# Rotary embedding on one core: cutting the last batch's store into 16, 12 and 4 KB a row, with the 4 KB in two DMAs of 126 and 2 partitions

## The chip, the cores and the metric

The kernel runs on one core of a Trainium2 chip. The metric is the device time of one execution in microseconds (us). Before the change it is 163.42 us, the median of three runs (163.31 to 163.57). The profile is one further execution, with a hardware profiler; its own time is 163.25 us, of which 161.4 us is the span from the first to the last instruction.

## The reference

Each head's 64 numbers are split into two halves of 32, and the halves are rotated by an angle that belongs to the position in the sequence. The input `x` is 8 x 2048 x 8 x 64 in float32, 33.5 MB; `cos` and `sin` are 2048 x 32.

```python
def reference(x, cos, sin):
    x1 = x[..., : x.shape[-1] // 2]
    x2 = x[..., x.shape[-1] // 2 :]
    cos = cos[None, :, None, :]
    sin = sin[None, :, None, :]
    out1 = x1 * cos - x2 * sin
    out2 = x1 * sin + x2 * cos
    return np.concatenate([out1, out2], axis=-1)
```

Each input number is read once and each output number written once, so some 67 MB cross between the device memory (HBM) and the on-chip memory, against a handful of multiplications and additions for each.

## The kernel before

**Layout.** A batch of `x` is laid over the 128 partitions: partition q holds 16 consecutive positions (`R`), each of 8 x 64 = 512 numbers (`HD`). One row, that is one partition of one batch, is 8192 numbers or 32 KB (`ROW`), contiguous in HBM and on the chip. `UNIT` is four positions, 8 KB a row. A whole batch is 4 MB.

**Loads.** Five buffers hold a batch each. `load` (line 64) puts the load of a batch on the queue of SyncE (SP), as one DMA of 32 KB a row, except that the first batch comes in 8, 8 and 16 KB a row. The load of batch b + 5 is issued after the work on batch b has been put in order (line 192), and SP waits before it until the store of batch b has left the buffer.

**Work.** `rotate` (line 101) handles one piece of a batch, 8 KB a row as a rule. In the common kind, "A", GpSimd (POOL) multiplies the swapped halves by `sin` and its negative (line 121), VectorE (DVE) multiplies the piece by `cos` (line 128) and adds the two in place (line 135). In five pieces, listed at line 98, the sum is made by TensorE with an identity matrix and copied back by ScalarE (ACT). None of these are in the last batch.

**Stores.** `shares` (line 176) says in which cuts a batch is stored, `pieces` (line 169) in which cuts it is computed. The main loop (line 183) computes a piece and then issues every store whose numbers are all done. `store` (line 70) puts it on the queue of ACT, but for the last batch on that of SP, whose loads are over by then. The last batch is computed in five pieces of 8, 8, 8, 4 and 4 KB a row, and stored in three cuts of 16, 8 and 8 KB a row: after the second piece, after the third, and after the fifth.

**Order.** `keep` keeps the marked instructions of an engine in the order in which they are written, so no scheduler moves them. Between engines and DMAs the order is made by semaphores. A DMA adds sixteen steps to its semaphore in all, as the transfer engines that carry its parts report. The program ends when the landings of all stores have been waited for, at the `TileContext`'s end.

**DMA.** A DMA is a list of rows. The sixteen transfer engines of the core carry it; the DMAs of SP and of ACT are two queues (q1 and q10 in the profile) on the same sixteen engines. In this kernel before the change every DMA has 128 rows. One row of a DMA shows in the trace as one packet; each of the sixteen engines carries eight rows.

Of the kernel before, what the change touches and what calls it, by code (L numbers as in the profile page):

```python
# [10 lines left out]
def kernel(  # L11
# [8 lines left out]
    keep = tc.keep_in_program_order  # L20
# [5 lines left out]
    P = 128  # L26
    HD = H * D
    R = S // P
    ROW = R * HD
    UNIT = 4 * HD  # L30
    NBUF = 5
    C = 512
    last = B - 1

    xv = x.rearrange("b (q r) h d -> b q (r h d)", q=P)
    ov = out.rearrange("b (q r) h d -> b q (r h d)", q=P)
# [19 lines left out]
    xts = {}  # L56
# [12 lines left out]

    def store(b, lo, n):  # L70
        queue = nc.sync if b == last else nc.scalar
        keep(queue.dma_start(out=ov[b, :, lo : lo + n], in_=xts[b][:, lo : lo + n]))

    keep(nc.scalar.dma_start(out=sin_sb, in_=sin_src))
    keep(nc.sync.dma_start(out=cos_sb, in_=cos_src))  # L75
# [3 lines left out]
    for mat, one in ((eye, 1.0), (neye, -1.0)):  # L79
        nc.gpsimd.memset(mat, 0.0)  # L80
        nc.gpsimd.affine_select(
            out=mat,
            in_=mat,
# [92 lines left out]
    def shares(b):  # L176
        if b == 0:
            return [2 * HD, 6 * HD, 2 * UNIT]
        if b == last:
            return [2 * UNIT, UNIT, UNIT]  # L180
        return [ROW]

    for b in range(B):
        done = 0
        outs = list(spans(shares(b)))
        for lo, n in spans(pieces(b)):
            rotate(b, lo, n)
            done = lo + n
            while outs and sum(outs[0]) <= done:
                store(b, *outs.pop(0))  # L190
        if b + NBUF <= last:
            load(b + NBUF)
# [30 lines left out]
```

## Time and profile before

| what | us |
|---|---|
| median of the runs (range) | 163.42 (163.31 to 163.57) |
| profiled execution | 163.25 |
| its span | 161.4 |
| busy in the span: DVE | 141.0 |
| busy in the span: POOL | 139.4 |
| busy in the span: PE (matmul) | 47.3 |
| busy in the span: ACT | 11.4 |
| busy share of the 16 DMA engines: q1 (SP) | 55.2% |
| busy share of the 16 DMA engines: q10 (ACT) | 42.7% |
| moved between HBM and chip | 67.65 MB, mean 419 GB/s |

The page cuts the span into 40 equal slices of about 4 us, and gives for each how busy the engines were and how much the DMA engines moved. The rows on DMA issues give the time from the issue of a transfer by its queue to its landing. The timeline lists the instructions with their start and length, in us from the start of the span. The view by stretches gives, for any stretch of the span, the busy time of PE, PEld, DVE, ACT and POOL, then the granted clock of TensorE, the mean busy share of the DMA engines and the GB/s that they moved. Below these views lie the packet records, one for each row that a transfer engine moved, with its queue, start, length and bytes, but without the number of the engine; and the times of the single semaphore steps.

### The profile page before, as it was taken

The page shows a single profiled execution, that of the slowest core. Times are in us where ns is not written, and L with a number is a line of the kernel's source. Part 1 is how long each engine was busy: PE and PEld are TensorE (multiplying, and loading weights), DVE is VectorE, ACT ScalarE, POOL GpSimd, SP SyncE. Part 2 cuts the span into 40 slices and gives each one's busy share as a digit, 9 for nine tenths or more (in the row PEclk, how much of TensorE's full clock was granted, in tenths as well). Part 3 has the DMA queues.
Part 4 walks back from the last instruction along what each step waited for, and adds up shares of the span by engine and source line. Part 5 has one row for each costly group of instructions (what it writes and reads, how often), then busy time and mean ns, then how long its engine had stood idle before and what let it go on. Part 6 is the DMA issues. An engine that isn't in the chain of part 4 may idle for free.

```text
span 161.4 us, 462 instructions
## 1 busy us (share of the span) xinstructions
PE 47.3 (29%) x80; PEld 17.9 (11%) x80; DVE 141.0 (87%) x68; ACT 11.4 (7%) x11; POOL 139.4 (86%) x72
## 2 busy tenths in 40 slices
PE   0000000397408770779029721974000000000000
PEld 0000000132003220223013301420000000000000
DVE  0668899999999999999999999999999998999900
ACT  0000000032200220020100220022000000000000
POOL 2299999999999899998995999998999979999200
PEclk9999999999975998589957995599655555555555
DMA  4999999999999999999999999999999999999995
GB/s 159 426 447 434 420 436 447 414 406 503 390 390 455 455 455 390 463 447 390 463 447 390 449 455 400 430 463 406 430 463 406 430 463 406 430 463 394 418 404 229
DMA packets 3458, 67.65 MB, mean 419 GB/s; under 512 B 384, under 2 KB 384, under 8 KB 768
## 3 DMA queue, kind: packets, MB, share of 16 engines
q1 hardware_dynamic: 2016, 38.01, 55.2%
q10 hardware_dynamic: 1440, 29.62, 42.7%
q14 instruction: 2, 0.02, 0.0%
HBM read 34.08 MB, written 33.55 MB: 419 GB/s over the span
## 4 chain that ended last, share of the span: by engine, by line
DVE 53%; DMA 27%; POOL 9%; issue 5%; SPq 0%; DVEq 0%; POOLq 0%
DVE t L128 28%; DMA xt<-in_x_dram 27%; DVE xt L135 22%; POOL t L121 9%; DVE t L147 3%; SPq L75 0%; DVEq L135 0%; POOLq L121 0%; SPq L67 0%
## 5 line engine op out<-in xcount | busy, mean ns | idle before, releaser
L121 POOL TENSOR_TENSOR t<-xt,sin_sb 128x1024 f32<-128x1024 f32 (+1 forms) x32 | 70.4, 2201 | 10.3 <-DMA xt<-in_x_dram 7.9
L128 DVE TENSOR_TENSOR t<-xt,cos_ps 128x2048 f32<-128x2048 f32 (+1 forms) x34 | 73.4, 2166 | 1.9 <-DMA xt<-in_x_dram 1.1
L121 POOL TENSOR_TENSOR t<-xt,nsin 128x1024 f32<-128x1024 f32 (+1 forms) x32 | 70.5, 2204 | 0.0
L135 DVE TENSOR_TENSOR xt<-t,t 128x2048 f32<-128x2048 f32 (+1 forms) x29 | 62.2, 2145 | 5.9 <-POOL t L121 3.4
L142 PE MATMUL o<-t,eye 128*128 128x512 f32 x24 | 16.0, 752 | 24.3 <-DVE t L128 20.8
L159 PE MATMUL o<-t,eye 128*128 128x512 f32 x16 | 11.3, 794 | 38.8 <-DVE t L128 36.6
L143 PE MATMUL o<-t,eye 128*128 128x512 f32 x24 | 14.7, 700 | 0.0
L144 ACT COPY xt<-o 128x1024 f32<-128x1024 f32 x6 | 6.1, 1012 | 45.7 <-PE o L143 45.7
L142 PEld LDWEIGHTS o<-t,eye 128*128 128x128 f32 x24 | 5.4, 248 | 33.5 <-issue 27.6
L159 PEld LDWEIGHTS o<-t,eye 128*128 128x128 f32 x16 | 3.7, 257 | 44.3 <-POOL t L121 30.7
L143 PEld LDWEIGHTS o<-t,eye 128*128 128x128 f32 x24 | 5.4, 227 | 7.5 <-issue 7.5
L160 PE MATMUL o<-t,neye 128*128 128x512 f32 x8 | 6.2, 863 | 0.2
L164 ACT COPY xt<-o 128x1024 f32<-128x1024 f32 x4 | 4.0, 1012 | 21.7 <-PE o L160 21.7
L90 DVE COPY cos_ps<-cos_sb 128x512 f32<-128x512 f32 x1 | 0.7, 694 | 4.4 <-DMA cos_sb<-in_cos_dram 4.4
L147 DVE TENSOR_TENSOR t<-xt,sin_ps 128x2048 f32<-128x2048 f32 x2 | 4.6, 2280 | 0.0
L160 PE MATMUL o<-t,eye 128*128 128x512 f32 x8 | 4.1, 592 | 0.0
L164 ACT ACT_TABLE_LOAD x1 | 1.3, 1283 | 32.9 <-DVE t L147 32.9
L160 PEld LDWEIGHTS o<-t,neye 128*128 128x128 f32 x8 | 1.9, 266 | 4.7 <-issue 3.1
L160 PEld LDWEIGHTS o<-t,eye 128*128 128x128 f32 x8 | 1.5, 190 | 1.9 <-issue 1.9
L92 DVE COPY sin_ps<-sin_sb 128x512 f32<-128x512 f32 x1 | 0.7, 689 | 0.0
L80 POOL MEMSET eye<- 128x128 f32 x1 | 0.2, 205 | 0.3 <-POOLq L207 0.3
L91 DVE TENSOR_SCALAR nsin<-sin_sb 128x512 f32<-128x512 f32 x1 | 0.4, 418 | 0.0
(7 smaller groups left out, 1.2 us busy)
## 6 DMA issues: line engine op xcount, KB each, us to landing
xt<-in_x_dram SPq DMA_DIRECT2D x7, 4096.0 KB, 39.0
out_dram<-xt ACTq DMA_DIRECT2D x6, 4096.0 KB, 28.4
xt<-in_x_dram SPq DMA_DIRECT2D x2, 1024.0 KB, 6.9
xt<-in_x_dram SPq DMA_DIRECT2D x1, 2048.0 KB, 12.3
out_dram<-xt ACTq DMA_DIRECT2D x1, 2048.0 KB, 25.1
out_dram<-xt SPq DMA_DIRECT2D x1, 2048.0 KB, 12.3
out_dram<-xt SPq DMA_DIRECT2D x2, 1024.0 KB, 8.7
out_dram<-xt ACTq DMA_DIRECT2D x1, 1536.0 KB, 19.9
```

The costliest lines, as they stand in the source:

```text
L90: keep(nc.vector.tensor_copy(cos_ps, cos_sb))
L92: keep(nc.vector.tensor_copy(sin_ps, sin_sb))
L121: nc.gpsimd.tensor_mul(out=t2u[:, :, u, :].rearrange("p (r h) d -> p r h d", h=H), in0=xu[:, :, 1 - u, :].rearrange("p (r h) d -> p r h d" ...
L128: nc.vector.tensor_mul(out=t1.rearrange("p (r k d) -> p r k d", r=nr, d=Dh), in0=xk, in1=rep(cos_ps[:, r0 : r0 + nr, :], 2 * H),)
L135: keep(nc.vector.tensor_add(out=xt, in0=t1, in1=t2))
L142: nc.tensor.matmul(oc, eye, t1[:, cs], start=True, stop=False)
L143: nc.tensor.matmul(oc, eye, t2[:, cs], start=False, stop=True)
L144: keep(nc.scalar.copy(xt[:, 2 * j * C : 2 * (j + 1) * C], o))
L147: nc.vector.tensor_mul(out=t2.rearrange("p (r k d) -> p r k d", r=nr, d=Dh), in0=xk, in1=rep(sin_ps[:, r0 : r0 + nr, :], 2 * H),)
L159: nc.tensor.matmul(oc, eye, t1u[:, gs, u, :], start=True, stop=False)
L160: nc.tensor.matmul(oc, eye if u else neye, t2u[:, gs, 1 - u, :], start=False, stop=True)
L164: nc.scalar.copy(xu[:, :, u, :], o.rearrange("p (g d) -> p g d", d=Dh))
```

## The change

Two things change, both for the last batch alone. The cuts of its store become 16, 12 and 4 KB a row in place of 16, 8 and 8: the second store now takes the third and fourth computed pieces, the last store the fifth alone. And the last store is issued as two DMAs on the same queue, one of partitions 0 to 125 and one of partitions 126 and 127. All other loads, stores and computations stay as they are and in their order. SP issues four stores at the end in place of three.

```diff
     def store(b, lo, n):
         queue = nc.sync if b == last else nc.scalar
-        keep(queue.dma_start(out=ov[b, :, lo : lo + n], in_=xts[b][:, lo : lo + n]))
+        cuts = (0, 126, P) if b == last and lo + n == ROW else (0, P)
+        for p, q in zip(cuts, cuts[1:]):
+            keep(
+                queue.dma_start(
+                    out=ov[b, p:q, lo : lo + n], in_=xts[b][p:q, lo : lo + n]
+                )
+            )
...
         if b == last:
-            return [2 * UNIT, UNIT, UNIT]
+            return [2 * UNIT, UNIT + 2 * HD, 2 * HD]
         return [ROW]
```

## The prediction

> **What bounds the kernel now.** I read the page first: its slices of the span and its list of DMA issues.
>
> ```profile
> span 161.4 us, 462 instructions
> DMA  4999999999999999999999999999999999999995
> GB/s 159 426 447 434 420 436 447 414 406 503 390 390 455 455 455 390 463 447 390 463 447 390 449 455 400 430 463 406 430 463 406 430 463 406 430 463 394 418 404 229
> ...
> HBM read 34.08 MB, written 33.55 MB: 419 GB/s over the span
> ...
> out_dram<-xt SPq DMA_DIRECT2D x1, 2048.0 KB, 12.3
> out_dram<-xt SPq DMA_DIRECT2D x2, 1024.0 KB, 8.7
> ```
>
> The DMA row is full from the second slice to the last but one: 16 transfer engines move about 420 GB/s throughout, and that bounds the kernel, whatever VectorE does. The second view is the timeline of the end, for when each store is handed over.
>
> ```profile
> 143.40 10.24 SPq L72 DMA_DIRECT2D out_dram<-xt  x3
> ...
> 148.13 1.23 DVE L128 TENSOR_TENSOR t<-xt,cos_ps 128x1024 f32<-128x1024 f32 x1
> 149.06 1.25 POOL L121 TENSOR_TENSOR t<-xt,nsin 128x512 f32<-128x512 f32 x1
> 149.46 1.23 DVE L135 TENSOR_TENSOR xt<-t,t 128x1024 f32<-128x1024 f32 x1
> 150.72 1.23 DVE L128 TENSOR_TENSOR t<-xt,cos_ps 128x1024 f32<-128x1024 f32 x1
> 152.05 1.23 DVE L135 TENSOR_TENSOR xt<-t,t 128x1024 f32<-128x1024 f32 x1
> ```
>
> The last sum ends at 153.28 us. The three stores of the last batch are issued at 143.40, 148.12 and 153.31 and land at 155.74, 158.19 and 160.59. The last two landings are 2.40 us apart and their issues 5.19: they do not follow the issues but queue behind one another. The third view, busy time by stretches of the end, shows how the queue runs out.
>
> ```profile
> 153.00:157.00 4.00, 0.00 (x0) 0.00 (x0) 0.28 (x1) 0.00 (x0) 0.00 (x0) 0.50 1.00 424
> 157.00:158.20 1.20, 0.00 (x0) 0.00 (x0) 0.00 (x0) 0.00 (x0) 0.00 (x0) 0.50 1.00 423
> 159.30:159.60 0.30, 0.00 (x0) 0.00 (x0) 0.00 (x0) 0.00 (x0) 0.00 (x0) 0.50 0.72 300
> 159.60:159.90 0.30, 0.00 (x0) 0.00 (x0) 0.00 (x0) 0.00 (x0) 0.00 (x0) 0.50 0.15 55
> 159.90:160.30 0.40, 0.00 (x0) 0.00 (x0) 0.00 (x0) 0.00 (x0) 0.00 (x0) 0.50 0.05 20
> ```
>
> The last two columns are the DMA share and GB/s. The engines work at share 1.00 until past 158.2 and then run dry one by one: in 159.9 to 160.3 the share 0.05 is less than one engine of sixteen. By the packet records, five engines finish their last share at 159.29 to 159.41, nine at 159.64 to 159.86, one at 159.95 and the last at 160.24. The sixteen landings follow 0.35 us later, at 159.66 to 160.59. So the end is set by one engine, 0.29 us behind the next and 0.38 behind the third; 0.84 us of closing work follow the landing (160.59 to 161.43).
>
> **Prices.** From the packet records: an 8 KB packet takes 309 ns and its successor on the same engine starts 306 ns after it; 4 KB is recorded at 159 ns, 12 KB at 460, 16 KB at 611. Less the same 3 ns, 4 KB costs 156 and 12 KB 457. One engine so moves 26.8 GB/s, sixteen 428.
>
> **Part 1: 16, 12, 4 instead of 16, 8, 8.** The second store now waits for the fourth of the batch's five rotations, not the third: it is issued at 150.70 instead of 148.12, 2.6 us later. On SP nothing but the last stores and the end stands behind it. Cover: the 16 KB store's packets keep each engine busy until 154.39 at the earliest, when the first 8 KB packet starts now. That leaves 3.7 us after the issue. Starting a queue from idle took 1.0 us (cos load issued at 0.73, first packet at 1.75). The 16 KB store itself took 4.0 (143.40 to 147.40), behind another queue's 32 KB packets; at that worst price the 12 KB would come at 154.70, 0.3 us late for the earliest engines alone, which have 0.95 us to spare against the last. The last pieces' data is ready when it was. Cost of the packets: 8 x (457 + 156) = 4.90 us an engine against 8 x (306 + 306) = 4.90. This part is worth 0.
>
> **Part 2: the 4 KB by two DMAs of 126 and 2 rows.** SP issues one more DMA, 0.34 us by its issue rows; the two leave by 154.0, and the queue reaches these rows after 154.39 + 8 x 0.457 = 158.05. Four us of cover, so nothing; without it, 0.34. The end waits for one landing more: a semaphore row of 17 ns, call it 0.02.
>
> How 126 rows are dealt to sixteen engines the trace doesn't show: every store in it has 128 rows in sixteen equal shares. If 126 were dealt unequally, the fullest engine would have 8 rows as now: 0. If one engine took all, 126 x 0.156 = 19.7 us. Every landing in the trace came in equal shares, and the most equal shares that 126 allows, up to sixteen, is 14 of 9. I take that: fourteen engines do a ninth packet, +0.16 us with its closing record, and two do none, -1.25 us. The 2 rows add one packet of 0.16 to each of two engines, which counts only if these are late ones. The Trainium skill ("DMA: Bandwidth & Descriptors", on why a DMA increments its semaphore by 16) has the rule: the largest number up to sixteen that divides the rows, on the lowest-numbered engines. By it 126 goes to engines 0 to 13 and 2 to engines 0 and 1; the sum would be the same, and no run here shows it yet.
>
> Then what a share of nine rows costs. The lower bound is 9 x 0.156, since none of the 128 packets of 4 KB took over 160 ns. But in that cut each engine has the same rows in every DMA, and nine-row shares must straddle the eight-row groups. The trace can't tell an engine's own limit (26.8 GB/s) from that of the path to its rows. If the path is the limit, an engine in another's rows takes turns: 312 ns a packet, for all nine +1.40 us. Between 0 and 1.40 the nearest row, the unstretched 4 KB, says 0, but for a cut that never mixes rows. I take two doubled packets, 0.31 us: the late group is 0.23 to 0.45 us behind the five early engines, about two packets, and so long neighbours are in the same rows. The Trainium skill ("SBUF — State Buffer", on the DMA port swizzle) speaks against the change here: four neighbouring partitions, and the four 32 further, share one port, at about 27 GB/s. Full sharing by that rule is the +1.40 above.
>
> **Sum.** The profiled execution took 163.25 us: span 161.43 and 1.82 around it. 163.25 + 0.16 + 0.31 + 0.02 = 163.74. It lies 0.17 under the median of the runs, 163.42; on their scale that is **163.9 us**, 0.3% slower. What a measurement can tell here is about 0.2%, 0.33 us: from 163.09 to 163.75 counts as no change.
>
> **Rivals.**
> *A, faster: the late engines are spared.* If the last engine and the next are the two with no row, the end is the third's, 159.86 + 0.16 = 160.02 instead of 160.24: -0.22 us, 163.2; if only the last is, 159.95 + 0.16 = 160.11, -0.13 and 163.3. For it: the lateness has a fixed cause. The two fetches of 8 KB on the instruction queue (at 91.53 and 98.82, 0.31 us each) come just before the last shares fall behind, and the first one's engine lost 0.53 us more in a packet of 1746 ns instead of 1213. From 112 us on the last landing trails by a steady 0.29 to 0.30. Such fetches may go to the same engines each time. Against: nothing says which engines these are, and two of sixteen by chance is 1 in 8. It decides only if the rows don't get in each other's way. To beat 0.2% the lateness must exceed this profile's; if the 0.17 us of the median were all such lateness, the gain could be 0.39, 163.0. The Trainium skill, in the same DMA page's table of latencies, calls engines 7 and 15 usually slower; by that the last one would be spared, but it is its best guess for another way of issuing.
> *B, no change: a ninth packet and nothing else.* 163.42 + 0.18 = 163.6. For it: every store packet after 155 us took 309 to 315 ns. Against: the new mixing of rows. If the late engines also get the two extra rows, 163.76.
> *C, much slower: rows collide in most packets*, or the two-row DMA's engines meet on one path at the very end. Five to nine doubled packets: 0.78 to 1.40, and the 0.18: 164.4 to 165.0. For it: if the rows are dealt in turns, fourteen neighbouring rows are wanted at once, and few paths serve them. Against: blocks of nine lie nine rows apart and in step would rarely meet.
>
> **How the numbers follow.** The forecast (one to four doubled packets, 163.75 to 164.4) 0.46; A 0.25, of which 0.11 under 163.09; B 0.18, of which 0.03 over 163.75; C 0.11. Faster 0.11; same 0.14 + 0.15 = 0.29; slower 0.46 + 0.03 + 0.11 = 0.60. The range 163.15 to 164.5 takes in B, the forecast, most of A and the foot of C; about 0.1 stays out on each side. The forecast's own range is 163.75 to 164.4.
>
> **What will show it.** In the profile after, VectorE's last sum should still end near 153.3, the issues stand at 143.4, 150.7, 153.3 and 153.65, and the DMA share stay at 1.00 until 158. The 12 KB store should land near 158.99 + 0.35 for the last engine. The 126 rows should land in fourteen steps: packets of 4 KB at 159 ns mean B or A, at up to 320 the forecast or C. Two engines should stop at 158.0 to 159.0, and in A the final landing comes before 160.5. I am wrong if 126 rows go to fewer engines, if the 12 KB store starts with the engines already empty, or if the late engines are not late in the next execution.

## The result, and the profile after

The changed kernel takes 164.19 us, the median of 13 runs, against 163.35 us for 13 runs of the kernel before beside them: +0.84 us. The ratio is 1.0057, with a 95% interval of 1.0035 to 1.0079. It also scatters more: 163.54 to 165.55 us, against 163.28 to 163.57. The profiled execution took 164.69 us and is thus one of the slower ones, 0.5 above the median; sizes read from its trace are to be taken with that in mind.

From the page of the changed kernel, the span, the DMA row of the 40 slices and the issues of the last batch's first two stores:

```profile
span 162.9 us, 463 instructions
...
DMA  5999999899899989989899999999999999999992
...
out_dram<-xt SPq DMA_DIRECT2D x1, 2048.0 KB, 12.4
...
out_dram<-xt SPq DMA_DIRECT2D x1, 1536.0 KB, 9.8
```

Up to the last slices nothing has changed, and the 16 KB store lands as before, 12.4 us after its issue. The 12 KB store, issued at 150.77, lands at 160.62. That is later than the end of *all* stores before (160.59), with the 4 KB still to come; the prediction had it at 158.99 + 0.35 = 159.34. Busy time by stretches of the end shows where it goes; the last two columns are the DMA engines' busy share and GB/s:

```profile
153.00:157.00 4.00, 0.00 (x0) 0.00 (x0) 0.34 (x1) 0.00 (x0) 0.00 (x0) 0.50 0.97 416
157.00:158.20 1.20, 0.00 (x0) 0.00 (x0) 0.00 (x0) 0.00 (x0) 0.00 (x0) 0.50 0.96 358
158.20:159.00 0.80, 0.00 (x0) 0.00 (x0) 0.00 (x0) 0.00 (x0) 0.00 (x0) 0.50 0.76 236
159.00:159.60 0.60, 0.00 (x0) 0.00 (x0) 0.00 (x0) 0.00 (x0) 0.00 (x0) 0.50 0.87 335
159.60:160.20 0.60, 0.00 (x0) 0.00 (x0) 0.00 (x0) 0.00 (x0) 0.00 (x0) 0.50 0.42 171
160.20:160.80 0.60, 0.00 (x0) 0.00 (x0) 0.00 (x0) 0.00 (x0) 0.00 (x0) 0.50 0.17 61
160.80:161.70 0.90, 0.00 (x0) 0.00 (x0) 0.00 (x0) 0.00 (x0) 0.00 (x0) 0.50 0.09 36
```

The same view of the kernel before, for four of these stretches:

```profile
157.00:158.20 1.20, 0.00 (x0) 0.00 (x0) 0.00 (x0) 0.00 (x0) 0.00 (x0) 0.50 1.00 423
158.20:159.00 0.80, 0.00 (x0) 0.00 (x0) 0.00 (x0) 0.00 (x0) 0.00 (x0) 0.50 0.97 410
159.60:160.20 0.60, 0.00 (x0) 0.00 (x0) 0.00 (x0) 0.00 (x0) 0.00 (x0) 0.50 0.11 41
160.20:160.80 0.60, 0.00 (x0) 0.00 (x0) 0.00 (x0) 0.00 (x0) 0.00 (x0) 0.50 0.00 0
```

The clear drop is from 158.2 to 159.0: 236 GB/s instead of 410. The view counts a packet where it starts, so its figure for a short stretch can mislead: the 358 of 157.0 to 158.2 looks like a loss, but experiment 1, which loses nothing, shows 352 there. With each packet of the packet records spread over its own length, the changed kernel moves 408 GB/s in that stretch and 288 in the next, against 427 and 428 before, and 430 and 423 in experiment 1. Then a tail remains: in the last 0.9 us the share 0.09 is one or two engines of sixteen.

The packet records say which packets these are. Of the 128 rows of 12 KB six are stretched, to between 633 and 1667 ns instead of 460; of the 128 rows of 4 KB eight are, to between 245 and 713 instead of 159. The other 242 have their usual length. A record has no engine number, but packets of one engine follow one another at fixed steps, and each engine closes its part of a DMA with a record of 4 bytes; by these the rows can be put together engine by engine. The sixteen engines start their 12 KB rows between 154.47 and 155.40. The engine that ends last starts at 154.80, in the middle of the field. Its last three 12 KB rows took 1186, 906 and 1058 ns, so that it was done with them at 160.27 instead of 158.46: 1.8 us lost. Then it did nine rows of 4 KB, each at 159 ns, and closed at 161.68. The engine that starts last, at 155.40, lost nothing: all its rows of 12 and 4 KB have their usual length, its part of the 12 KB store landed at 159.44, it did nine rows of 4 KB, and it closed at 160.46. Before, the last engine closed at 160.24. So of the 1.44 us between the two ends 0.22 are on the engine that was late anyway, 0.16 of it for the ninth row, and 1.22 come from a middle engine that was held up and overtaken. Two engines did no 4 KB row and stopped at 158.35 and 158.45; they are from the middle of the field too.

### The profile page after: what moved, and what is told of

It is laid out like the page before. It is cut to its first block, busy times and chain, and to the rows that moved or that the text cites. A ratio compares the mean times of both kernels' runs of the same rounds, so it can differ in the third digit from the quotient of the medians.

```text
span 162.9 us, 463 instructions
## 1 busy us (share of the span) xinstructions
PE 49.6 (30%) x80; PEld 18.7 (11%) x80; DVE 141.0 (87%) x68; ACT 11.4 (7%) x11; POOL 139.4 (86%) x72
## 4 chain that ended last, share of the span: by engine, by line
DVE 52%; DMA 27%; POOL 9%; issue 5%; SPq 0%; DVEq 0%; POOLq 0%
DVE t L134 28%; DMA xt<-in_x_dram 27%; DVE xt L141 21%; POOL t L127 9%; DVE t L153 3%; SPq L81 0%; DVEq L141 0%; POOLq L127 0%; SPq L67 0%
## 5 line engine op out<-in xcount | busy, mean ns | idle before, releaser
L148 PE MATMUL o<-t,eye 128*128 128x512 f32 x24 | 17.2, 805 | 22.9 <-DVE t L134 19.5
L165 PE MATMUL o<-t,eye 128*128 128x512 f32 x16 | 12.1, 847 | 38.5 <-DVE t L134 36.3
L149 PE MATMUL o<-t,eye 128*128 128x512 f32 x24 | 14.9, 709 | 0.0
L166 PE MATMUL o<-t,eye 128*128 128x512 f32 x8 | 4.1, 592 | 0.0
## 6 DMA issues: line engine op xcount, KB each, us to landing
out_dram<-xt SPq DMA_DIRECT2D x1, 2048.0 KB, 12.4
```

Of the source, the lines that this page charges most:

```text
L148: nc.tensor.matmul(oc, eye, t1[:, cs], start=True, stop=False)
L149: nc.tensor.matmul(oc, eye, t2[:, cs], start=False, stop=True)
L165: nc.tensor.matmul(oc, eye, t1u[:, gs, u, :], start=True, stop=False)
L166: nc.tensor.matmul(oc, eye if u else neye, t2u[:, gs, 1 - u, :], start=False, stop=True)
```

## The experiments

The theory after the result: a cut of 126 rows is dealt so that engines read partitions which in the 128-row cuts belong to other engines, and where the two cuts meet in time both sides are held up (crossing). Which partitions an engine reads isn't in the trace, so crossing can only be tested by what it makes of the time and of the packets. Its rivals: the recut to 16, 12, 4 itself; the uneven count (a ninth row); the second DMA and its issue; and, for crossing, whether it happens on the chip or in HBM. All diffs are against the changed kernel. Medians of "before" are from runs beside each group: 163.34 for the first four, 163.32 for the next four, 163.28 for the last three.

**1. The recut alone.**

```diff
-        cuts = (0, 126, P) if b == last and lo + n == ROW else (0, P)
+        cuts = (0, P)
```

> Edit: the cuts 16, 12, 4 are kept, the last 4 KB is one DMA of 128 rows. Crossing theory (nine-row shares reach into the rows of other engines and both sides are stretched): nothing crosses, 163.35 +- 0.15, all 4 KB packets at 159 ns. Recut theory (the later 12 KB store is the cost): about 164.2. Ninth-row theory (the uneven count is the cost): also 163.35.

Measured 163.33 us; ratio 0.9994 (0.9984 to 1.0003). Its end by stretches:

```profile
157.00:158.20 1.20, 0.00 (x0) 0.00 (x0) 0.00 (x0) 0.00 (x0) 0.00 (x0) 0.50 0.83 352
158.20:159.00 0.80, 0.00 (x0) 0.00 (x0) 0.00 (x0) 0.00 (x0) 0.00 (x0) 0.50 1.04 430
159.00:159.60 0.60, 0.00 (x0) 0.00 (x0) 0.00 (x0) 0.00 (x0) 0.00 (x0) 0.50 0.75 307
159.60:160.20 0.60, 0.00 (x0) 0.00 (x0) 0.00 (x0) 0.00 (x0) 0.00 (x0) 0.50 0.25 102
160.20:160.80 0.60, 0.00 (x0) 0.00 (x0) 0.00 (x0) 0.00 (x0) 0.00 (x0) 0.50 0.02 7
```

By the packet records no 4 or 12 KB packet is stretched, so the 0.83 and the 1.04 are the counting by starts; the work is gone by 160.4. The 12 KB store is issued 2.6 us later and costs nothing; it lands at 159.53. The whole loss is in the split by rows.

**2. Two DMAs of 112 and 16 rows.**

```diff
-        cuts = (0, 126, P) if b == last and lo + n == ROW else (0, P)
+        cuts = (0, 112, P) if b == last and lo + n == ROW else (0, P)
```

> Edit: the last 4 KB in two DMAs of 112 and 16 rows in place of 126 and 2. If both are dealt in sixteen equal shares (7 rows and 1), each engine has 8 packets as before the change, but in blocks that do not fit the eight-row groups. Crossing theory: slower than before the change by 0.3 to 2 us, with stretched packets of 4 and 12 KB. Ninth-row theory: 163.35, since nobody has a ninth. Two-DMA theory (the second issue is the cost): about 164.2, without stretched packets.

Measured 164.54 us; ratio 1.0058 (1.0040 to 1.0076). Both DMAs landed in sixteen steps, so no engine was left out. Twenty 4 KB packets and seven 12 KB packets are stretched, the longest to 1787 ns. The loss doesn't need a ninth row.

**3. Two DMAs of 64 rows.** The same line with 64 in place of 126.

> Edit: two DMAs of 64 rows each. Equal count (4 + 4 packets). Crossing theory: each half of the partitions is read by all sixteen engines, two for each eight-row group, so slower by 0.5 to 1.5 us, with stretched packets. Ninth-row theory: 163.35. Two-DMA theory: about 164.2, without stretched packets.

Measured 163.82 us; ratio 1.0026 (1.0012 to 1.0039). The sign is as expected and there are nine stretched packets of each size, but the size, 0.48 us by the medians, is just under the range. The profiled execution, at 164.57 us, is the slowest of the twelve. 119 of the 128 packets of 4 KB have their usual length.

**4. Two DMAs of 128 rows of 2 KB.**

```diff
-        cuts = (0, 126, P) if b == last and lo + n == ROW else (0, P)
+        cuts = (0, P)
...
-            return [2 * UNIT, UNIT + 2 * HD, 2 * HD]
+            return [2 * UNIT, UNIT + 2 * HD, HD, HD]
```

> Edit: the last 4 KB in two DMAs of 128 rows of 2 KB, so one more DMA than before the change, but every engine in its own rows. Crossing theory: 163.35 +- 0.2. Two-DMA theory: about 164.2. Ninth-row theory: 163.35.

Measured 163.38 us; ratio 0.9999 (0.9991 to 1.0008), and no packet is stretched. A second DMA as such costs nothing, though its issue took 1.20 us (153.88 to 155.08) where a single one takes 0.34.

**5. The split on 8 KB.**

```diff
-            return [2 * UNIT, UNIT + 2 * HD, 2 * HD]
+            return [2 * UNIT, UNIT, UNIT]
```

> Edit: the cuts are 16, 8, 8 as before the change, and the last 8 KB is split into 126 and 2 rows. Crossing theory, if the cost grows with the bytes that cross: twice the +0.84 us of the change, about 165.0. If it is set by how far the engines are out of step alone: again about 164.2. Ninth-row theory (the uneven count is the cost): 0.31 us for a ninth row of 8 KB, 163.7.

Measured 164.94 us; ratio 1.0098 (1.0081 to 1.0115). +1.62 us against +0.84: about twice, as expected if the cost grows with the bytes that cross. It is one comparison, and the cut ahead is 8 KB here instead of 12, so the bytes alone aren't shown to be the reason. Thirty packets of 8 KB are stretched, by 7.0 us in sum; in the changed kernel it was 5.5 us in sum.

**6. Two DMAs of 120 and 8 rows.** The line of experiment 2 with 120.

> Edit: the last 4 KB in 120 and 8 rows. Equal shares would be fifteen of 8 and eight of 1. Crossing theory: slower, 163.8 to 164.8, with stretched packets of 4 and 12 KB. If the engines that are late by the instruction fetches were among those left without a row, faster than before the change by up to 0.2. The late engines' number of 4 KB packets (0, 8 or 9) tells in which group they are.

Measured 164.15 us; ratio 1.0041 (1.0026 to 1.0056), with seventeen stretched packets of 4 KB and ten of 12 KB. The last step of the 120-row DMA (162.23) is followed by the last of the 8-row DMA at 162.42: the last engine did nine rows, so it is one of the eight that carry the 8 rows. The last but one (162.07) has no such follower: it did eight. These are the engines that end last, after being held up; the one that starts its 12 KB rows last (155.45) again has them all at usual length, did nine rows of 4 KB and closed at 160.51.

**7. The rows written elsewhere in HBM, by a destination of 16 x 8 rows.** The last 4 KB is one DMA of 128 rows, with the rows of its destination in another order.

```diff
+        dst = ov[b, :, lo : lo + n]
+        if b == last and lo + n == ROW:
+            row = dst.ap[0][0]
+            dst = dataclasses.replace(dst, ap=[[row, 16], [16 * row, 8], dst.ap[1][:]])
+        keep(queue.dma_start(out=dst, in_=xts[b][:, lo : lo + n]))
```

> Edit: the last 4 KB is one DMA of 128 rows, but its row of partition 8a + c is written to the place of row a + 16c in HBM (so the last 4 KB of the rows of the last batch are written in another order than the reference's). Crossing theory on the on-chip side: each engine still reads its own partitions, so 163.35 +- 0.2 and no stretched packets. Crossing theory on the HBM side: each engine writes rows that lie where other engines' rows lay, so slower by 0.3 us or more with stretched packets.

Measured 164.06 us; ratio 1.0044 (1.0030 to 1.0057), with seven stretched packets of 4 KB and eight of 12 KB. By the expectation this spoke for the HBM side. But the edit had changed two things, the places (neighbouring rows now go 16 rows, 512 KB, apart) and the shape (16 x 8 rows instead of 128), and the shape may change how the rows are dealt to the engines. So the two sides had to be taken apart with shapes that stay as they were.

**8. The split in the middle.**

```diff
-        cuts = (0, 126, P) if b == last and lo + n == ROW else (0, P)
+        cuts = (0, 126, P) if b == last and n == 2 * HD else (0, P)
...
-            return [2 * UNIT, UNIT + 2 * HD, 2 * HD]
+            return [2 * UNIT, 2 * HD, UNIT + 2 * HD]
```

> Edit: the cuts are 16, 4, 12, and the 4 KB in the middle is the one in 126 and 2 rows; the last 12 KB has 128 rows. Crossing theory: the engines that were held up have nothing to make it up with, and the 12 KB rows of the early ones meet the 4 KB rows of the late ones: 163.9 to 164.6. If only the last piece matters, because the end follows it: 163.35.

Measured 165.20 us; ratio 1.0109 (1.0094 to 1.0123), above the range that I gave. The 4 KB rows now cross both the 16 KB rows ahead of them (three are stretched, up to 1328 ns instead of 611) and the 12 KB rows behind (seven), and 28 of the 4 KB rows themselves. The end isn't a special place: rows are held up at both borders.

**9. The same shape, written 36 rows back.** `rows` is the output with batch and partition as one index. Experiments 10 and 11 are the same edit with other numbers.

```diff
-        cuts = (0, 126, P) if b == last and lo + n == ROW else (0, P)
+        cuts = (0, P)
+        rows = ov.rearrange("b q n -> (b q) n")
         for p, q in zip(cuts, cuts[1:]):
+            at = b * P - (36 if b == last and lo + n == ROW else 0)
             keep(
                 queue.dma_start(
-                    out=ov[b, p:q, lo : lo + n], in_=xts[b][p:q, lo : lo + n]
+                    out=rows[at + p : at + q, lo : lo + n], in_=xts[b][p:q, lo : lo + n]
```

> Edit: the last 4 KB is one DMA of 128 rows with the same shape as in the recut alone, but partition q is written to the row 36 before its own in HBM (rows 92 to 127 of batch 6 and 0 to 91 of batch 7, so those rows end in other numbers than the reference's, and the last 4 KB of the last 36 rows stay unwritten). On the chip every engine keeps its own partitions, in HBM each engine writes where other engines' rows lay. On-chip theory: 163.35 +- 0.2, no stretched packets. HBM theory: slower by 0.3 us or more, with stretched 12 KB packets.

Measured 163.28 us; ratio 0.9997 (0.9989 to 1.0006):

```profile
158.20:159.00 0.80, 0.00 (x0) 0.00 (x0) 0.00 (x0) 0.00 (x0) 0.00 (x0) 0.50 0.80 328
159.00:159.60 0.60, 0.00 (x0) 0.00 (x0) 0.00 (x0) 0.00 (x0) 0.00 (x0) 0.50 0.88 362
159.60:160.20 0.60, 0.00 (x0) 0.00 (x0) 0.00 (x0) 0.00 (x0) 0.00 (x0) 0.50 0.22 89
160.20:160.80 0.60, 0.00 (x0) 0.00 (x0) 0.00 (x0) 0.00 (x0) 0.00 (x0) 0.50 0.00 0
```

All is over by 160.3, and not one packet is stretched. (The share counts a packet where it starts, so it moves a little between neighbouring stretches.) With this shift, rows that land among other engines' rows in HBM cost nothing.

**10. The split of 126 and 2 rows, written to batch 0.** The same edit with cuts of 126 kept, and 896 (seven batches) in place of 36.

> Edit: the 126 and 2 rows of the change, written to the same rows of batch 0 in place of batch 7 (28 MB away; batch 0's last 4 KB a row are overwritten and batch 7's stay unwritten). Partitions cross as in the change; in HBM the rows lie far from those that the 12 KB store is writing. On-chip theory: as slow as the change, 164.0 to 164.4. HBM theory, if it is nearness to the other rows that hurts: 163.35 to 163.6; if it is the position of a row within a batch (the same for all batches): as slow as the change.

Measured 164.09 us; ratio 1.0043 (1.0026 to 1.0060):

```profile
157.00:158.20 1.20, 0.00 (x0) 0.00 (x0) 0.00 (x0) 0.00 (x0) 0.00 (x0) 0.50 0.94 355
158.20:159.00 0.80, 0.00 (x0) 0.00 (x0) 0.00 (x0) 0.00 (x0) 0.00 (x0) 0.50 0.79 277
159.60:160.20 0.60, 0.00 (x0) 0.00 (x0) 0.00 (x0) 0.00 (x0) 0.00 (x0) 0.50 0.52 191
160.20:160.80 0.60, 0.00 (x0) 0.00 (x0) 0.00 (x0) 0.00 (x0) 0.00 (x0) 0.50 0.17 68
```

The pattern of the change is back, 28 MB away from the 12 KB rows: 277 GB/s from 158.2 to 159.0, then the tail, with nineteen stretched packets of 4 KB and seven of 12 KB.

**11. The control: 128 rows, written to batch 0.** One DMA, 896 rows back.

> Edit: the last 4 KB as one DMA of 128 rows, each written to its own row of batch 0 in place of batch 7 (the control of the other two; the same rows are overwritten and left unwritten). Every theory: 163.35 +- 0.2.

Measured 163.34 us; ratio 1.0004 (0.9993 to 1.0015), no packet stretched.

Experiments 9 to 11 speak for the chip's side of the transfer: with 128 rows in one DMA, moving them by 36 rows or to another batch in HBM is free; with 126 and 2 rows, the loss is there in another batch too. What the slow kernels share is how the partitions are cut. Experiment 7 stays open: its loss can come from the shape or from the order of its rows in HBM, which is another one than in experiments 9 to 11, and no run tells the two apart. The profiled executions in one table, packets from 153 us on that took over 16 ns longer than usual. The packets belong to the one profiled execution, whose time stands beside them; where rows are held up, it differs from the median:

| last pieces | stretched packets | sum of the excess, us | this execution, us | median, us |
|---|---|---|---|---|
| 16, 12, 4 by 128 rows (1) | 0 | 0 | 163.40 | 163.33 |
| 16, 12, 2, 2 by 128 rows (4) | 0 | 0 | 163.53 | 163.38 |
| 128 rows, 36 back (9) | 0 | 0 | 163.27 | 163.28 |
| 128 rows, batch 0 (11) | 0 | 0 | 163.32 | 163.34 |
| 64 + 64 rows (3) | 18 | 5.4 | 164.57 | 163.82 |
| 16 x 8 rows in another order (7) | 15 | 4.6 | 164.42 | 164.06 |
| 126 + 2 rows, batch 0 (10) | 26 | 5.6 | 164.12 | 164.09 |
| 120 + 8 rows (6) | 27 | 9.2 | 165.10 | 164.15 |
| 126 + 2 rows (the change) | 14 | 5.5 | 164.69 | 164.19 |
| 112 + 16 rows (2) | 27 | 7.5 | 164.54 | 164.54 |
| 126 + 2 rows of 8 KB (5) | 30 | 7.0 | 165.49 | 164.94 |
| 4 KB in 126 + 2, then 12 KB (8) | 38 | 9.3 | 165.10 | 165.20 |

No execution without stretched packets is slow, and none with them is as fast as before. The sum of the excess doesn't give the time, though: what counts is how far a single engine is held up.

## Why the prediction was right

The forecast was 163.9 us, slower by crossing rows, in a range of 163.15 to 164.5; measured were 164.19, within the forecast's own 163.75 to 164.4. That it came so near is in part luck, as the term for crossing shows. By its steps:

- *The recut is worth 0.* So it was: 0.9994 in experiment 1. Issues 3.7 us ahead of their place in the queue are covered.
- *One more issue is hidden.* It was, though at three times the price that I gave: the two issues that end the program last 1.47 us, of which the second takes 1.03, not 0.34. From the timeline of SP at the end of the changed kernel (start, length):

```profile
153.37 1.47 SPq L75 DMA_DIRECT2D out_dram<-xt  x2
```

 The four us of cover took it. The closing wait was costed at 0.02 us and didn't show. SP's waits at the end are, after as before, three landings of the stores; they sum to 7.0 us against 6.7, but the longest is now 4.7, since the 12 KB store comes in so late:

```profile
SPq L224 <- DMA out_dram<-xt: 7.0, 3, 4.7
```

- *126 rows go to fourteen engines, nine each.* The 126-row DMA landed in fourteen late steps, and two engines carried no row of 4 KB. That is the Trainium skill's rule ("DMA: Bandwidth & Descriptors", on why a DMA increments its semaphore by 16), and this trace agrees with its count; which engines they are by number, the trace doesn't tell.
- *+0.16 us for a ninth row.* It is on the last engine's path in the profiled execution. It isn't what makes the loss: 112 and 16 rows, with eight for each engine, lose no less.
- *Two doubled packets, +0.31 us.* That rows get in each other's way was right; the size of the term and the place where it acts were not. It was added to the path of the last engine of before and to its 4 KB rows, with long neighbours as the reason. In the profiled execution the engine that starts last lost nothing, and an engine from the middle lost 1.8 us in three rows of 12 KB and became the last. The signs named before the run asked about the lengths of packets of 4 KB alone; of these eight are stretched, to 245 to 713 ns, some near a doubled 312 and some far above, and the dearest row is one of 12 KB, at 1667 ns instead of 460. By the medians, +0.84 less 0.16 leaves about 0.7 us for this term, over twice what I took.
- *Rival A, the late engines are spared.* No. The two engines that start their 12 KB rows last (155.16 and 155.40) were late again, and each carried nine rows of 4 KB, all at usual length. They closed at 160.21 and 160.46, against 159.95 and 160.24 before. Sparing two engines of the middle of the field wins nothing. In experiment 6, too, the one that starts last was not spared. The trace gives no engine a number, so it can't say whether the late ones are those that the prediction named.
- *Rival B, a ninth packet and nothing else (163.6)* falls with the 14 stretched packets. (Its store packets after 155 us took up to 316 ns, not 315.) *Rival C (five to nine doubled packets, 164.4 to 165.0)* is near what the slower executions did, 164.69 in the profile; two of the thirteen, 165.18 and 165.55, are beyond it. I had tied it to how the rows are dealt; the runs show instead that the loss varies from one execution to the next of the same program.

The rule that I had set against the change, that partitions four by four share a port ("SBUF — State Buffer", on the DMA port swizzle, in the Trainium skill), pointed the right way: experiments 9 to 11 speak for the chip's side. At full strength it isn't seen. By it, as an estimate from that page, each half of the partitions reaches half of the ports, so the two DMAs of 64 rows would have taken up to twice as long, +1.25 us for eight rows of 0.156; measured were 0.48, with 119 of 128 packets of usual length. It is an upper bound, since the engines start these rows up to 0.9 us apart and aren't all in the same half at once. That ports are what the engines wait for, no run shows; it stays open.

## What to carry to other kernels

In this kernel the queue of DMAs that bounds it ran at full rate as long as each of its stores took all 128 partitions in their order; a cut by rows cost more than the imbalance that it was to mend. Where a store has to be cut, try first to cut it along the row (16, 12, 4 or 16, 12, 2, 2: free here), and leave the 128 partitions whole. Before giving some engines less to do, find out whether the late ones are among them.

## What the runs showed of the hardware that I had not expected

- The stretch begins before the rows that cause it are seen to move: the first long 12 KB packet of the changed kernel starts at 157.09, the first 4 KB packet at 158.13. That row's usual end, 157.55, is still 0.6 us ahead of the first 4 KB record. The engines may be at work on a row well before its record begins; that is inferred, not shown.
- The engine that starts its 12 KB rows last was not held up in them, in the changed kernel nor in experiments 2, 3, 6 and 10 (the five executions in which its rows were followed one by one). Being late is not what gets an engine held up.
- The last of two DMAs issued one behind the other at the end took 1.03 us (2 rows, in the changed kernel) and 1.20 us (128 rows, experiment 4) to issue, against 0.34 for a single one. That isn't so for every pair: the first loads of the kernel before, also issued one behind the other, took 0.43 to 0.53 us each. The reason for the difference stays open.
- The split made the time uncertain as well as longer: 163.54 to 165.55 us over 13 runs, a spread of 2.0 us against 0.3 for the 13 runs before; the widest group of runs of the kernel before (23 runs, beside experiments 9 to 11) has 0.8.
- One DMA of 128 rows with a destination given as 16 x 8 rows loses 0.4% (experiment 7): for this store the shape of the access or the order of its rows in HBM matters, not only its bytes.
